# Earlier loads of the scaled SSD output tiles, and one wide stationary block for dt, in a hybrid encoder layer

## The chip, the cores and the metric

The kernel runs on one NeuronCore of a Trainium2 chip. The metric is the device time of one execution in microseconds, as the median of several runs. Engines are called TensorE (PE in the profile, its weight loads PEld), VectorE (DVE), ScalarE (ACT), GpSimd (POOL) and SyncE (SP, which here only issues DMAs).

## The reference

One encoder layer in fp32 is applied to two requests of 256 tokens each, with 1024 channels. Each request goes through a half-step SwiGLU FFN (1024 to 2816 and back), then three branches on the normalised input `u`, then a second FFN:

```
u = rms_norm(x);  q,k,v,q_mem,z,xbc,dt_raw,gates = split(u @ w_in)
A: neighbourhood attention    B: bidirectional Mamba-2 SSD    C: attention into 256 memory tokens
dt_f, dt_b = softplus(dt_raw + bias) ;  a = -exp(a_log)          # 32 heads each, 64 columns in all
y_ssd = ssd(x, dt_f, a_f, B, C) + flip(ssd(flip ...)) + d * x ;  o_ssd = grouped_rms_norm(y_ssd * silu(z))   # 8 groups
merged = sum_b sigmoid(gate_b) * (branch_b @ w_br_b) ;  x = x + merged @ w_out
```

## The kernel before, in words

**Products.** Both requests stand side by side as 512 columns, so tiles are 128 channels by 512 tokens. Every fp32 operand is split into a high part (rounded to fp32r, names ending in h) and the remainder (ending in l), and a product is three fp32r matmuls: high by high, high by low, low by high (`unit`, L535, lines L545 to L547). A unit with 8 blocks of 128 rows is 24 matmuls into one PSUM bank. There are eight banks: five in pool `pm` (names m, q, ac), three in pool `pd` for everything else.

**Weights.** `fetch` (L281) loads weight tiles of up to 128x1024 (`wr`) into a ring of nine, through SP's DMA queue. `ahead` (L312) splits the tiles up to two items ahead: ACT copies to fp32r (`wh`, L322), DVE subtracts for the remainder (`wl`, L236), into pools of three buffers. The subtraction frees the ring slot.

**Order.** `make_plan` (L71) lists the units of TensorE in order. `run` (L361) takes them one after the other. After each unit the last unit's result is evacuated, and `step` (L332) moves each active side task (a generator) to its next `yield` and starts at most one task from a queue. At the `ssd` gates it steps twice per unit (L372), with up to four active tasks (L1029). The instruction order of each engine, SP's DMA issues included, is fixed when the program is built and depends on this order; each engine works in order.

**SSD.** `t_ssd` (L1232) is the side task of a group: decay rows `e` (ACT) are multiplied by dt and by C·B products on DVE, and TensorE turns them into y (L1305). At the end come a sum, a reciprocal root on DVE, and for groups 6 and 7 a diagonal (dg, L514) that TensorE spreads to `R` (L523). For groups 0 to 5 (`KEEP`) the two output tiles go to DRAM (`scr_o`), and so does the factor of the norm (`scr_n`).

**What comes after the last group.** Eight gate units of 24 matmuls (kind `gate`, branch `ssd`, `do_gate` L1026; their tanh `tg` on ACT frees the bank), then 16 units of the branch product (`bs`, L1094) that read all 16 output tiles as pairs `osh`, `osl`. Side task `t_os` (L1340) makes these pairs: for groups 0 to 5 it loads the factor row (`rw`, L1343) and each tile (`or`, L1349), scales the tile on DVE (L247) and splits it (ACT `osh` L258, DVE `osl` L236). It has no step of its own: load, scaling and split are issued at once, tile after tile. Groups 0 to 3 are queued at the first gate (L1029), groups 4 to 7 at the first `bs` unit (L1074).

**dt.** `do_dt` (L1131) is a unit with 64 columns of weights, so 24 matmuls whose result has 64 partitions. `t_dt` (L1138) adds the bias, computes softplus by a series on 64x512 tiles, multiplies by `-exp(a_log)`, then transposes both results in eight 64-row transposes (L1166, L1167) and copies them to `tokd` (128 tokens by four blocks of 128).

**Start.** `warm` (L422) fills a tile on POOL (L425), lets ACT write one column of it (its table load comes first), and runs 16 matmuls on it (L429), 32 passes in the trace, before the first real product (L609).

Of the kernel before, what the change touches and what calls it, by code (L numbers as in the profile page):

```python
# [16 lines left out]
KD = 8  # L17
# [153 lines left out]
PCOLS = {}  # L171
_n = 0
for _name, _w in (("ffn1", 8), ("mix", 8), ("mem", 8), ("ffn2", 8), ("cw", 160), ("cb", 32), ("qn", 1), ("kn", 1),
                  ("mqn", 2), ("mkn", 2), ("sn", 16), ("dd", 16), ("dtb", 1), ("al", 1)):
    PCOLS[_name] = _n
    _n += _w
NPAR = _n
# [7 lines left out]
class Layer:  # L185
# [126 lines left out]
    def ahead(self, ci):  # L312

        for i in range(self.n_split, min(ci + 3, len(ITEMS))):
            it = ITEMS[i]
            self.fetch(i + self.depth)
            self.sums(i + 1)
            n = it.nk * it.m
            t = self.live[it.src]
            hi = self.pw.tile([128, 1024], F32R, tag="hi", name=self.name("wh"))  # L320
# [56 lines left out]
    def setup(self):  # L377
# [3 lines left out]
        dma = nc.sync.dma_start  # L381
# [20 lines left out]
        self.ident, self.ones, self.gele, self.lege = c(0), c(1), c(3, 2), c(6, 2)  # L402
        self.tri = (c(2, 2), c(4, 2))
        self.namask = c(8)[:, :64].rearrange("p (n k) -> p n k", n=2)
        self.lots = self.pc.tile([128, 4, 64], F32, name="lots")
        self.half = self.pc.tile([128, 32], F32, name="half")
        self.merged, self.gus = [None] * 8, {}
# [14 lines left out]
    def warm(self):  # L422

        z = self.g(p="af")
        self.G.memset(z, 0.0)  # L425
        self.act(z[:, :1], z[:, 1:2], AF.Copy)
        ps = self.bank("wm")
        for _ in range(WARM):
            self.T.matmul(ps[:, :256], z[:, :128], z[:, :256], start=True, stop=True)  # L429
# [699 lines left out]


    def do_dt(self, key, cis):  # L1131
        ps = self.unit(cis, self.u, m=64)

        def evac():
            self.later("dt", self.t_dt(ps))
        return evac

    def t_dt(self, ps):  # L1138
        V, S, T = self.V, self.S, self.T
        r = slice(0, 64)  # L1140
        v, m, e, z, w = (self.g(p="dt") for _ in range(5))
        self.act(v[r], ps[r], AF.Identity, bias=self.par("dtb", 0, r))
        self.ts(m[r], v[r], 0.0, ALU.max)
        self.stt(e[r], v[r], -1.0, v[r], ALU.mult, ALU.min)
        self.act(e[r], e[r], AF.Exp)
        yield
        self.ts(w[r], e[r], 2.0, ALU.add)
        V.reciprocal(w[r], w[r])
        self.tt(z[r], e[r], w[r], ALU.mult)
        yield  # L1150
        self.tt(w[r], z[r], z[r], ALU.mult)
        self.ts(e[r], w[r], 1.0 / 15, ALU.mult)
        for k in (13, 11, 9, 7, 5, 3):
            self.stt(e[r], e[r], 1.0 / k, w[r], ALU.add, ALU.mult)
            if k == 9:
                yield
        self.stt(e[r], e[r], 1.0, z[r], ALU.add, ALU.mult)
        self.stt(v[r], e[r], 2.0, m[r], ALU.mult, ALU.add)
        ea = self.small(2, "ea")
        self.act(ea[r, 0:1], self.par("al", 0, r), AF.Exp)  # L1160
        self.ts(w[r], v[r], ea[r, 0:1], ALU.mult, -1.0, ALU.mult)
        yield
        ps = self.bank("dtT")
        for t in range(4):
            s = slice(t * 128, (t + 1) * 128)
            T.transpose(ps[:, t * 128:t * 128 + 64], v[r, s], self.ident[r, 0:64])  # L1166
            T.transpose(ps[:, t * 128 + 64:(t + 1) * 128], w[r, s], self.ident[r, 0:64])  # L1167
        tk = self.pc.tile([128, 4, 128], F32, name="tokd")
        V.tensor_copy(tk.rearrange("p t c -> p (t c)"), ps)
        self.tok = tk  # L1170
# [167 lines left out]
        self.stt(v, v, self.half[:, 2 * g + i:2 * g + i + 1], r, ALU.mult, ALU.mult)  # L1338

    def t_os(self, g):  # L1340
        if g < KEEP:
            r, sn = self.g(p="rw"), self.scr_n
            self.nc.sync.dma_start(out=r, in_=bass.AP(sn.tensor, sn.offset + g * 512, [[0, 128], [1, 512]]))  # L1343
        for i in range(2):
            k = 2 * g + i
            t = self.oraw.pop(k, None)
            if t is None:
                t = self.g(p="or")
                self.nc.sync.dma_start(out=t, in_=self.scr_o[k])  # L1349
                self.scale_o(g, i, t, r)  # L1350
            self.os[k] = self.split_tile(t, "os")
        return
        yield


def layer_kernel(tc, aps):
# [7 lines left out]
def layout(inp):  # L1364
# [15 lines left out]
    def put(name, arr):  # L1380
        p[:arr.shape[0], PCOLS[name]:PCOLS[name] + arr.shape[1]] = arr
# [14 lines left out]
    put("dtb", np.concatenate([f("dt_bias_f")[0], f("dt_bias_b")[0]])[:, None])  # L1396
    put("al", np.concatenate([f("a_log_f")[0], f("a_log_b")[0]])[:, None])

    i = np.arange(128)
    c = np.zeros((128, NCONST), np.float32)  # L1400
# [2 lines left out]
    for k, t in enumerate(tri):  # L1403
# [17 lines left out]
    return {"w": w, "xT": chan("x_prompt", "x_sample"), "memT": chan("mem_prompt", "mem_sample"), "params": p,  # L1421
            "consts": c, "strip": np.ascontiguousarray(strip.reshape(8, 128, 512))}


# [19 lines left out]
```

## Time and profile before

| | |
|---|---|
| median of three runs (lowest, highest) | 1757.79 us (1756.99, 1758.3) |
| the profiled execution | 1756.64 us; its span 1754.9 us |
| granted TensorE clock, mean over the span | 0.998 |
| busy: TensorE, weight loads, DVE, ACT | 1737.2, 1419.9, 1234.6, 848.0 us |
| moved by DMA | 209.69 MB, mean 119 GB/s |

The span runs from the first to the last instruction; the time of the execution adds what lies around it. The busy times overlap, since the engines run side by side. Matmuls are pipelined, so a matmul's row is longer than the distance to the next one; what a matmul costs is read from start to start. In a row of the timeline, the bracket at the end says how long the engine had been idle before it, and what ended that.

### The profile page before, as it was taken

The numbers are of one execution on the slowest core, as the hardware profiler recorded it, in microseconds if no ns is written. First come the engines' busy times: TensorE is split into PE (matmuls) and PEld (weight loads), VectorE is DVE, ScalarE is ACT, GpSimd is POOL, SyncE is SP. The second block draws the span as 40 slices with busy tenths as digits, with TensorE's granted clock in tenths as the row PEclk, the third lists the DMA queues.
The fourth block names the chain that finished last, engine by engine and source line by source line (L and its number), as shares of the span: only waits on it lengthen the run. The fifth ranks groups of instructions, "written<-read, shape, count | busy, mean of one in ns | idle before, by whom it ended". The sixth has DMA issues, their size and how long they took to land.

```text
span 1754.9 us, 22611 instructions
## 1 busy us (share of the span) xinstructions
PE 1737.2 (99%) x8568; PEld 1419.9 (81%) x8568; DVE 1234.6 (70%) x2056; ACT 848.0 (48%) x1515; POOL 0.7 (0%) x5
## 2 busy tenths in 40 slices
PE   9999999999999999999999999999899999999999
PEld 7888888988788888788877777777688878888887
DVE  7676776876544467835778888888753697776775
ACT  6443443543224336533666766766532464444442
POOL 0000000000000000000000000000000000000000
PEclk9999999999999999999999999999999999999999
DMA  6144233442323232333344545446433234244331
GB/s 258 60 143 144 97 107 134 155 156 89 96 77 104 88 103 85 102 109 97 120 127 127 132 139 136 123 138 175 162 126 121 84 109 138 79 153 127 99 115 48
DMA packets 79708, 209.69 MB, mean 119 GB/s; under 512 B 11120, under 2 KB 19696, under 8 KB 79600
## 3 DMA queue, kind: packets, MB, share of 16 engines
q1 hardware_dynamic: 79600, 208.26, 37.6%
q8 instruction: 67, 1.10, 0.3%
q14 instruction: 41, 0.34, 0.1%
HBM read 198.64 MB, written 9.58 MB: 119 GB/s over the span
## 4 chain that ended last, share of the span: by engine, by line
PE 96%; DVE 2%; DMA 1%; ACT 1%; issue 0%; SPq 0%; DVEq 0%; ACTq 0%
PE ac L567 20%; PE m L545 10%; PE m L546 10%; PE m L547 10%; PE q L589 5%; PE q L591 5%; PE q L590 5%; PE m L1094 5%; PE d L546 5%; PE d L547 5%; PE d L545 5%; PE y L1305 2%; PE hT L692 1%; PE CB L1255 1%; PE q L609 1%; PE q L611 1%
## 5 line engine op out<-in xcount | busy, mean ns | idle before, releaser
L322 ACT CAST wh<-wr 128x1024 fp32r<-128x1024 f32 (+1 forms) x357 | 371.2, 1040 | 686.5 <-PE ac L567 167.1
L236 DVE TENSOR_TENSOR wl<-wr,wh 128x1024 fp32r<-128x1024 f32 (+1 forms) x357 | 431.5, 1209 | 264.4 <-ACT wh L322 259.4
L545 PE MATMUL m<-uh,wh 128*128 128x512 f32 (+1 forms) x584 | 234.9, 402 | 6.7 <-ACT tg L251 6.7
L567 PE MATMUL ac<-wh,sh 128*128 128x512 f32 (+1 forms) x616 | 229.4, 373 | 0.5 <-ACT wh L322 0.5
L546 PE MATMUL m<-ul,wh 128*128 128x512 f32 (+1 forms) x584 | 229.6, 393 | 0.0
L567 PE MATMUL ac<-wl,sh 128*128 128x512 f32 (+1 forms) x616 | 228.1, 370 | 0.7 <-DVE wl L236 0.7
L547 PE MATMUL m<-uh,wl 128*128 128x512 f32 (+1 forms) x584 | 228.5, 391 | 0.0
L567 PE MATMUL ac<-wh,sl 128*128 128x512 f32 (+1 forms) x616 | 228.0, 370 | 0.0
L545 PEld LDWEIGHTS m<-uh,wh 128*128 128x128 f32 (+1 forms) x584 | 109.6, 188 | 38.3 <-ACT tg L251 6.9
L546 PE MATMUL d<-hl,wh 128*128 128x512 f32 x352 | 137.2, 390 | 0.7 <-DVE hl L236 0.7
L545 PE MATMUL d<-hh,wh 128*128 128x512 f32 x352 | 137.4, 390 | 0.5 <-ACT hh L258 0.5
L547 PE MATMUL d<-hh,wl 128*128 128x512 f32 x352 | 137.0, 389 | 0.0
L567 PEld LDWEIGHTS ac<-wl,sh 128*128 128x128 f32 x616 | 116.1, 188 | 20.6 <-DVE wl L236 1.3
L567 PEld LDWEIGHTS ac<-wh,sh 128*128 128x128 f32 x616 | 116.0, 188 | 20.6 <-ACT wh L322 1.3
L567 PEld LDWEIGHTS ac<-wh,sl 128*128 128x128 f32 x616 | 116.0, 188 | 19.7
L547 PEld LDWEIGHTS m<-uh,wl 128*128 128x128 f32 (+1 forms) x584 | 109.6, 188 | 24.6 <-issue 0.4
L546 PEld LDWEIGHTS m<-ul,wh 128*128 128x128 f32 (+1 forms) x584 | 109.7, 188 | 23.6 <-issue 1.5
L247 DVE SCALAR_TENSOR_TENSOR x<-d,x 128x512 f32<-128x512 f32 x96 | 66.2, 690 | 76.5 <-PE d L547 76.0
L589 PE MATMUL q<-wh,uh 128*128 128x512 f32 x256 | 102.9, 402 | 0.0
L236 DVE TENSOR_TENSOR wr<-wr,wr 128x1024 f32<-128x1024 f32 x80 | 97.6, 1221 | 6.3 <-DMA wr<-in_w 5.3
L591 PE MATMUL q<-wl,uh 128*128 128x512 f32 x256 | 99.9, 390 | 0.0
L590 PE MATMUL q<-wh,ul 128*128 128x512 f32 x256 | 99.9, 390 | 0.0
(253 smaller groups left out, 2857.6 us busy)
## 6 DMA issues: line engine op xcount, KB each, us to landing
wr<-in_w SPq DMA_DIRECT2D x308, 512.0 KB
rw<-scr_r SPq DMA_DIRECT2D x64, 256.0 KB
nv<-scr_v SPq DMA_DIRECT2D x64, 64.0 KB
scr_o<-cv SPq DMA_DIRECT2D x12, 256.0 KB
or<-scr_o SPq DMA_DIRECT2D x12, 256.0 KB
wr<-in_w SPq DMA_DIRECT2D x9, 256.0 KB
x<-in_xT SPq DMA_DIRECT2D x8, 256.0 KB
mr<-in_memT SPq DMA_DIRECT2D x8, 256.0 KB
```

Of the source, the lines that this page charges most:

```text
L236: self.V.tensor_tensor(out=out, in0=a, in1=b, op=op)
L247: self.V.scalar_tensor_tensor(out=out, in0=a, scalar=s, in1=b, op0=op0, op1=op1)
L322: self.S.copy(hi[:, :n], t[:, :n])
L545: self.T.matmul(ps[:m], wh[:, kk, :], xh, start=i == 0, stop=False)
L546: self.T.matmul(ps[:m], wh[:, kk, :], xl, start=False, stop=False)
L547: self.T.matmul(ps[:m], wl[:, kk, :], xh, start=False, stop=i == n - 1)
L567: go = lambda l, r, **f: self.T.matmul(ps, l, r, skip_group_check=True, **f)
L589: self.T.matmul(self.qb[t], xh, wh[:, kk, :], start=k == 0, stop=False)
L590: self.T.matmul(self.qb[t], xl, wh[:, kk, :], start=False, stop=False)
L591: self.T.matmul(self.qb[t], xh, wl[:, kk, :], start=False, stop=k == KD - 1)
L1094: go = lambda l, r, **f: self.T.matmul(ps, l, r, skip_group_check=True, **f)
L1305: T.matmul(yb[64 * hp:64 * hp + 64, b * 256:(b + 1) * 256], xt[i][:, (2 * b + st) * 128 + 64 * hp:(2 * b + st) * 128 + 64 * hp + 64], w[hp ...
```

## The change

Three things change.

1. `t_os` issues the loads of a group's row and two tiles, yields twice, and only then scales both tiles and splits them. For groups 6 and 7, whose tiles are still on the chip, the split comes at once.
2. For dt, `ahead` puts the high and the low part of the weights side by side in one 128-column stationary block per 128 rows. High by high and low by high are one matmul with 128 output partitions, and high by low a second one with 64. `t_dt` first copies the result out, transposes it in four full transposes, adds both halves and the bias row, and computes softplus on 128 partitions by 256. Bias and `a_log` come as rows, broadcast to all partitions by one DMA at setup (`dtrow`).
3. In `warm`, ACT's column is written in a small tile of its own, filled after the big one, so the matmuls no longer read what ACT writes.

```diff
@@ ahead
+            if it.m == 64:
+                both = self.pw.tile([128, 1024], F32R, tag="hi", name=self.name("wh"))
+                v = both.rearrange("p (k m) -> p k m", k=it.nk)
+                raw = t[:, :n].rearrange("p (k m) -> p k m", k=it.nk)
+                self.S.copy(v[:, :, :64], raw)
+                self.tt(v[:, :, 64:], raw, v[:, :, :64].bitcast(F32), ALU.subtract)
...
@@ setup
+        self.tok = self.pc.tile([128, 4, 128], F32, name="tokd")
+        self.dtrow = self.pc.tile([128, 128], F32, name="dtrow")
+        rows = self.a["dtrow"]
+        dma(out=self.dtrow, in_=bass.AP(rows.tensor, rows.offset, [[0, 128], [1, 128]]))
@@ warm
         self.G.memset(z, 0.0)
-        self.act(z[:, :1], z[:, 1:2], AF.Copy)
+        y = self.small(2, "wm")
+        self.G.memset(y, 0.0)
+        self.act(y[:, :1], y[:, 1:], AF.Copy)
@@ do_dt
-        ps = self.unit(cis, self.u, m=64)
+        ps = self.bank()
+        ci, = cis
+        self.ahead(ci)
+        w = self.split.pop(ci)
+        for k in range(KD):
+            xh, xl = self.u[k]
+            self.T.matmul(ps, w[:, k, :], xh, start=k == 0, stop=False, skip_group_check=True)
+            self.T.matmul(ps[:64], w[:, k, :64], xl, start=False, stop=k == KD - 1, skip_group_check=True)
@@ t_dt (the series itself is as before, on 128x256)
-        v, m, e, z, w = (self.g(p="dt") for _ in range(5))
-        self.act(v[r], ps[r], AF.Identity, bias=self.par("dtb", 0, r))
+        raw = self.g(p="dt")
+        S.copy(raw, ps)
+        yield
+        ps = self.bank("dtT")
+        for t in range(4):
+            c = slice(t * 128, (t + 1) * 128)
+            T.transpose(ps[:, c], raw[:, c], self.ident)
+        v, m, e, z, w = (self.g(p="dt")[:, :256] for _ in range(5))
+        self.tt(four(v), four(ps)[:, :, 0:64], row(0), ALU.add)
+        self.tt(four(v), four(ps)[:, :, 64:128], four(v), ALU.add)
...
-        self.act(ea[r, 0:1], self.par("al", 0, r), AF.Exp)
-        self.ts(w[r], v[r], ea[r, 0:1], ALU.mult, -1.0, ALU.mult)
-        yield
-        ps = self.bank("dtT")
-        for t in range(4):
-            s = slice(t * 128, (t + 1) * 128)
-            T.transpose(ps[:, t * 128:t * 128 + 64], v[r, s], self.ident[r, 0:64])
-            T.transpose(ps[:, t * 128 + 64:(t + 1) * 128], w[r, s], self.ident[r, 0:64])
-        tk = self.pc.tile([128, 4, 128], F32, name="tokd")
-        V.tensor_copy(tk.rearrange("p t c -> p (t c)"), ps)
+        self.stt(tk[:, :, 0:64], four(e), 2.0, four(m), ALU.mult, ALU.add)
+        self.act(self.dtrow[:, 64:], self.dtrow[:, 64:], AF.Exp)
+        self.stt(tk[:, :, 64:128], tk[:, :, 0:64], -1.0, row(1), ALU.mult, ALU.mult)
@@ t_os
+        ks = (2 * g, 2 * g + 1)
         if g < KEEP:
             r, sn = self.g(p="rw"), self.scr_n
             self.nc.sync.dma_start(out=r, in_=bass.AP(sn.tensor, sn.offset + g * 512, [[0, 128], [1, 512]]))
-        for i in range(2):
-            k = 2 * g + i
-            t = self.oraw.pop(k, None)
-            if t is None:
-                t = self.g(p="or")
-                self.nc.sync.dma_start(out=t, in_=self.scr_o[k])
-                self.scale_o(g, i, t, r)
-            self.os[k] = self.split_tile(t, "os")
-        return
-        yield
+            for k in ks:
+                self.oraw[k] = self.g(p="or")
+                self.nc.sync.dma_start(out=self.oraw[k], in_=self.scr_o[k])
+            yield
+            yield
+            for i in range(2):
+                self.scale_o(g, i, self.oraw[ks[i]], r)
+        for k in ks:
+            self.os[k] = self.split_tile(self.oraw.pop(k), "os")
```

The first place where rows move is ACT's queue during the last gate units. `tg_..<-m_..` is a gate's tanh, `osh` the cast of an output tile, `wh` that of a weight tile, `yq` and `e` belong to the last SSD groups. Before, from the fifth early tile to the seventh gate's tanh:

```order
L258 CAST osh_10877<-or_10874 128x512
L322 CAST wh_11103<-wr_10555 128x1024
L251 ACTIVATE yq_11033<-cv_10453 128x512
L258 CAST osh_10884<-or_10881 128x512
L322 CAST wh_11136<-wr_10557 128x1024
L258 CAST osh_10915<-or_10912 128x512
L258 CAST osh_10922<-or_10919 128x512
L251 ACTIVATE tg_10957<-m_10824 128x512
L251 ACTIVATE tg_11020<-m_10926 128x512
L251 ACTIVATE tg_11066<-m_10989 128x512
L251 ACTIVATE tg_11131<-m_11035 128x512
L251 ACTIVATE tg_11164<-m_11100 128x512
```

With the change, from the third gate's tanh to the eighth early tile:

```order
L251 ACTIVATE tg_10929<-m_10796 128x512
L251 ACTIVATE e_10936<-e_10936 128x256
L251 ACTIVATE e_10964<-rw_10860,lots 128x256 x2
L251 ACTIVATE e_10936<-rw_10860,lots 128x128
L258 CAST osh_10946<-or_10856 128x512
L251 ACTIVATE e_10936<-rw_10860,lots 128x128
L251 ACTIVATE e_10964<-e_10964 128x512
L258 CAST osh_10950<-or_10858 128x512
L251 ACTIVATE e_10936<-e_10936 128x256
L332 CAST wh_11030<-wr_10545 128x1024
L258 CAST osh_10973<-or_10894 128x512
L258 CAST osh_10977<-or_10896 128x512
```

The tanh of the third gate (tg_10957 before, tg_10929 now) stood behind the casts of all eight early tiles and now stands ahead of the last four; those of the fourth to sixth gate follow behind the next weight cast after the piece shown.

The second place is SP's queue in the same stretch. `or` are output tiles, `rw` rows of the norm (scr_n) or of the SSD (scr_r), `wr` weight tiles. Before, from the fifth early tile to the eighth:

```order
L1349 DMA or_10874<-scr_o 128x512
L290 DMA wr_11101<-in_w 128x1024
L1349 DMA or_10881<-scr_o 128x512
L290 DMA wr_11134<-in_w 128x1024
L1349 DMA or_10912<-scr_o 128x512
L1343 DMA rw_11230<-scr_n 128x512
L1343 DMA rw_11277<-scr_n 128x512
L290 DMA wr_11169<-in_w 128x1024
L1349 DMA or_10919<-scr_o 128x512
```

With the change, from an SSD row to the first weight loads after the eighth early tile:

```order
L1254 DMA rw_10829<-scr_r 128x512
L1369 DMA rw_10854<-scr_n 128x512
L1254 DMA rw_10860<-scr_r 128x512
L1372 DMA or_10856<-scr_o 128x512
L1372 DMA or_10858<-scr_o 128x512
L1369 DMA rw_10892<-scr_n 128x512
L1372 DMA or_10894<-scr_o 128x512
L1372 DMA or_10896<-scr_o 128x512
L290 DMA wr_10982<-in_w 128x1024
L290 DMA wr_11028<-in_w 128x1024
L290 DMA wr_11093<-in_w 128x1024
L290 DMA wr_11126<-in_w 128x1024
```

Before, a weight load stood ahead of each of these tiles; now the fifth to eighth tile (or_10856 to or_10896) stand together, ahead of the weight loads (wr_10982 is the tile that was wr_10990). The loads of the first four early tiles likewise stand together, a few rows higher up.

The third place is the dt unit on TensorE. Before, the first six of 24 rows:

```order
L545 MATMUL m_3790<-uh_3206,wh_3724 64x512
L546 MATMUL m_3790<-ul_3207,wh_3724 64x512
L547 MATMUL m_3790<-uh_3206,wl_3725 64x512
L545 MATMUL m_3790<-uh_3213,wh_3724 64x512
L546 MATMUL m_3790<-ul_3214,wh_3724 64x512
L547 MATMUL m_3790<-uh_3213,wl_3725 64x512
```

With the change, the first six of 16:

```order
L1155 MATMUL m_3794<-uh_3211,wh_3729 128x512
L1156 MATMUL m_3794<-ul_3212,wh_3729 64x512
L1155 MATMUL m_3794<-uh_3218,wh_3729 128x512
L1156 MATMUL m_3794<-ul_3219,wh_3729 64x512
L1155 MATMUL m_3794<-uh_3259,wh_3729 128x512
L1156 MATMUL m_3794<-ul_3260,wh_3729 64x512
```

The third row of each block of 128 is gone, and the first has 128 output partitions.

## Rows read from the trace of the kernel before

**Rows 1.** The page's busy times in us (share of the span, number of instructions).

```profile
PE 1737.2 (99%) x8568; PEld 1419.9 (81%) x8568; DVE 1234.6 (70%) x2056; ACT 848.0 (48%) x1515; POOL 0.7 (0%) x5
```

**Rows 2.** All that TensorE waited for from 1196 to 1300 us: us in total, times, longest.

```profile
PE m L545 <- ACT tg L251: 6.7, 1, 6.7
PE R L523 <- DVE dg L514: 0.5, 1, 0.5
```

**Rows 3.** Timeline of the last gate units, by engine: start in us, duration in us, engine, line, operation, tiles, count, idle before.

```profile
1261.53 0.33 SPq L290 DMA_DIRECT2D wr<-in_w  x1
1261.92 2.52 SPq L1349 DMA_DIRECT2D or<-scr_o  x2
...
1265.77 0.75 DVE L247 SCALAR_TENSOR_TENSOR or<-or,half,rw 128x512 f32<-128x512 f32 x1 [1.68 <-DMA or<-scr_o]
...
1266.56 0.62 ACT L258 CAST osh<-or 128x512 fp32r<-128x512 f32 x1 [3.74 <-DVE or L247]
1267.08 2.54 ACT L251 ACTIVATE tg<-m 128x512 f32<-128x512 f32 x5
...
1259.87 1.13 PE L523 MATMUL R<-dg,consts 128*128 128x128 f32 x8 [0.48 <-DVE dg L514]
1267.72 0.79 PE L545 MATMUL m<-uh,wh 128*128 128x512 f32 x1 [6.72 <-ACT tg L251]
...
1271.26 0.39 PE L547 MATMUL m<-uh,wl 128*128 128x512 f32 x1
```

**Rows 4.** The second half of the stall, and the stretch after it: length, busy us (instructions) of PE, PEld, DVE, ACT, POOL, then the granted clock, the DMA share and GB/s.

```profile
1264.40:1267.70 3.30, 0.00 (x0) 0.00 (x0) 1.24 (x2) 1.14 (x3) 0.00 (x0) 0.50 0.49 160
1267.70:1271.26 3.56, 3.54 (x9) 2.81 (x9) 0.20 (x1) 1.92 (x4) 0.00 (x0) 0.51 0.00 0
```

**Rows 5.** SP's queue some 30 us earlier, as a timeline: the first and the last of five issues.

```profile
1230.98 0.33 SPq L290 DMA_DIRECT2D wr<-in_w  x1
...
1233.27 0.44 SPq L1349 DMA_DIRECT2D or<-scr_o  x1
```

**Rows 6.** Timeline of DVE, and of TensorE at two groups of y matmuls, in the same stretch.

```profile
1239.70 0.69 DVE L236 TENSOR_TENSOR osl<-or,osh 128x512 fp32r<-128x512 f32 x1
1240.31 0.48 DVE L247 SCALAR_TENSOR_TENSOR e<-e,tokd,ca 128x256 f32<-128x256 f32 x1
1240.70 0.61 DVE L247 SCALAR_TENSOR_TENSOR e<-e,tokd,cb 128x128 f32<-128x128 f32 x2
1241.23 1.22 DVE L236 TENSOR_TENSOR wl<-wr,wh 128x1024 fp32r<-128x1024 f32 x1
1242.37 0.42 DVE L236 TENSOR_TENSOR e<-e,e 128x256 f32<-128x256 f32 x1
...
1243.10 0.74 DVE L247 SCALAR_TENSOR_TENSOR or<-or,half,rw 128x512 f32<-128x512 f32 x1
...
1239.33 0.65 PE L1305 MATMUL y<-e,xt 128*64 128x256 f32 x2
1239.90 0.50 PE L546 MATMUL m<-ul,wh 128*128 128x512 f32 x1
...
1243.57 1.08 PE L1305 MATMUL y<-e,xt 128*64 128x256 f32 x6
```

**Rows 7.** What the weight casts on ACT waited for from 1196 to 1300 us, the largest entry.

```profile
ACT wh L322 <- PE m L546: 15.4, 7, 5.2
```

**Rows 8.** Timeline of TensorE around the dt unit and the unit behind it, around dt's transposes, and around four full transposes elsewhere.

```profile
455.53 0.40 PE L545 MATMUL m<-uh,wh 128*64 128x512 f32 x1
...
461.05 0.39 PE L589 MATMUL q<-wh,uh 128*128 128x512 f32 x1
...
466.49 0.39 PE L589 MATMUL q<-wh,uh 128*128 128x512 f32 x1
...
493.78 0.27 PE L1166 MATMUL dtT<-consts,dt 64*128 64x64 f32 x1
...
494.42 0.50 PE L589 MATMUL q<-wh,uh 128*128 128x512 f32 x1
...
402.79 1.18 PE L836 MATMUL tr<-consts,kr 128*128 128x128 f32 x8
403.72 0.48 PE L589 MATMUL q<-wh,mgh 128*128 128x512 f32 x1
```

**Rows 9.** DVE's copy of dt's result as a timeline row, and the stretch from 440 to 520 us with the columns of rows 4.

```profile
494.52 0.69 DVE L1169 COPY tokd<-dtT 128x512 f32<-128x512 f32 x1 [3.42 <-PE dtT L1167]
...
440.00:520.00 80.00, 80.00 (x374) 64.42 (x373) 42.49 (x67) 21.53 (x39) 0.00 (x0) 1.00 0.29 88
```

**Rows 10.** The start as a timeline, and two stretches of the warm-up matmuls alone (length, PE, PEld, clock, DMA share, GB/s).

```profile
0.73 0.52 POOL L425 MEMSET af<- 128x512 f32 x1 [0.29 <-POOLq L1428]
...
2.02 0.20 ACT L251 ACTIVATE af<-af 128x1 f32<-128x1 f32 x1
...
2.28 10.11 PE L429 MATMUL wm<-af 128*128 128x256 f32 x32 [2.28 <-ACT af L251]
...
7.56 1.23 DVE L236 TENSOR_TENSOR wl<-wr,wh 128x1024 fp32r<-128x1024 f32 x1 [0.84 <-ACT wh L322]
...
2.28:8.28 6.00, 6.00 (x14) 4.79 (x15) 1.00 0.94 321
8.28:12.04 3.76, 3.76 (x19) 3.27 (x18) 1.00 1.03 404
```

More of the change, by code (lines that the diff above doesn't have):

```diff
@@ L173 @@
 for _name, _w in (("ffn1", 8), ("mix", 8), ("mem", 8), ("ffn2", 8), ("cw", 160), ("cb", 32), ("qn", 1), ("kn", 1),
-                  ("mqn", 2), ("mkn", 2), ("sn", 16), ("dd", 16), ("dtb", 1), ("al", 1)):
+                  ("mqn", 2), ("mkn", 2), ("sn", 16), ("dd", 16)):
     PCOLS[_name] = _n
@@ L319, in ahead @@
             t = self.live[it.src]
+            if it.m == 64:
[4 more added lines that the diff above has]
+                self.tt(v[:, :, 64:], raw, v[:, :, :64].bitcast(F32), ALU.subtract)
+                self.drop(it.src)
+                self.split[i] = v
+                self.n_split = i + 1
+                continue
             hi = self.pw.tile([128, 1024], F32R, tag="hi", name=self.name("wh"))
@@ L1140, in t_dt @@
         r = slice(0, 64)
-        v, m, e, z, w = (self.g(p="dt") for _ in range(5))
-        self.act(v[r], ps[r], AF.Identity, bias=self.par("dtb", 0, r))
-        self.ts(m[r], v[r], 0.0, ALU.max)
-        self.stt(e[r], v[r], -1.0, v[r], ALU.mult, ALU.min)
-        self.act(e[r], e[r], AF.Exp)
-        yield
-        self.ts(w[r], e[r], 2.0, ALU.add)
-        V.reciprocal(w[r], w[r])
-        self.tt(z[r], e[r], w[r], ALU.mult)
-        yield
[L1151 to L1159, printed above, removed]
-        self.act(ea[r, 0:1], self.par("al", 0, r), AF.Exp)
-        self.ts(w[r], v[r], ea[r, 0:1], ALU.mult, -1.0, ALU.mult)
+        four = lambda z: z.rearrange("p (t c) -> p t c", t=4)
+        raw = self.g(p="dt")
+        S.copy(raw, ps)
         yield
@@ L1164, in t_dt @@
         for t in range(4):
-            s = slice(t * 128, (t + 1) * 128)
-            T.transpose(ps[:, t * 128:t * 128 + 64], v[r, s], self.ident[r, 0:64])
-            T.transpose(ps[:, t * 128 + 64:(t + 1) * 128], w[r, s], self.ident[r, 0:64])
-        tk = self.pc.tile([128, 4, 128], F32, name="tokd")
-        V.tensor_copy(tk.rearrange("p t c -> p (t c)"), ps)
-        self.tok = tk
+            c = slice(t * 128, (t + 1) * 128)
+            T.transpose(ps[:, c], raw[:, c], self.ident)
+        v, m, e, z, w = (self.g(p="dt")[:, :256] for _ in range(5))
+        tk = self.tok
+        row = lambda i: self.dtrow[:, 64 * i:64 * i + 64].unsqueeze(1).to_broadcast([128, 4, 64])
+        self.tt(four(v), four(ps)[:, :, 0:64], row(0), ALU.add)
+        self.tt(four(v), four(ps)[:, :, 64:128], four(v), ALU.add)
+        self.ts(m, v, 0.0, ALU.max)
+        self.stt(e, v, -1.0, v, ALU.mult, ALU.min)
+        self.act(e, e, AF.Exp)
+        yield
+        self.ts(w, e, 2.0, ALU.add)
+        V.reciprocal(w, w)
+        self.tt(z, e, w, ALU.mult)
+        yield
+        self.tt(w, z, z, ALU.mult)
+        self.ts(e, w, 1.0 / 15, ALU.mult)
+        for k in (13, 11, 9, 7, 5, 3):
+            self.stt(e, e, 1.0 / k, w, ALU.add, ALU.mult)
+            if k == 9:
+                yield
+        self.stt(e, e, 1.0, z, ALU.add, ALU.mult)
+        self.stt(tk[:, :, 0:64], four(e), 2.0, four(m), ALU.mult, ALU.add)
+        self.act(self.dtrow[:, 64:], self.dtrow[:, 64:], AF.Exp)
+        self.stt(tk[:, :, 64:128], tk[:, :, 0:64], -1.0, row(1), ALU.mult, ALU.mult)
         yield
@@ L1343, in t_os @@
             self.nc.sync.dma_start(out=r, in_=bass.AP(sn.tensor, sn.offset + g * 512, [[0, 128], [1, 512]]))
-        for i in range(2):
-            k = 2 * g + i
-            t = self.oraw.pop(k, None)
-            if t is None:
-                t = self.g(p="or")
-                self.nc.sync.dma_start(out=t, in_=self.scr_o[k])
-                self.scale_o(g, i, t, r)
-            self.os[k] = self.split_tile(t, "os")
-        return
-        yield
+            for k in ks:
+                self.oraw[k] = self.g(p="or")
+                self.nc.sync.dma_start(out=self.oraw[k], in_=self.scr_o[k])
+            yield
+            yield
+            for i in range(2):
+                self.scale_o(g, i, self.oraw[ks[i]], r)
+        for k in ks:
+            self.os[k] = self.split_tile(self.oraw.pop(k), "os")
 def layer_kernel(tc, aps):
@@ L1395, in layout @@
     put("dd", cols(np.repeat(f("ssd_d")[0], 64)))
-    put("dtb", np.concatenate([f("dt_bias_f")[0], f("dt_bias_b")[0]])[:, None])
-    put("al", np.concatenate([f("a_log_f")[0], f("a_log_b")[0]])[:, None])
+    dtrow = np.concatenate([f(n)[0] for n in ("dt_bias_f", "dt_bias_b", "a_log_f", "a_log_b")])
     i = np.arange(128)
@@ L1420, in layout @@
     strip = strip.reshape(8, 2, 128, 256).transpose(0, 2, 1, 3)
-    return {"w": w, "xT": chan("x_prompt", "x_sample"), "memT": chan("mem_prompt", "mem_sample"), "params": p,
+    return {"w": w, "xT": chan("x_prompt", "x_sample"), "memT": chan("mem_prompt", "mem_sample"), "params": p, "dtrow": dtrow,
             "consts": c, "strip": np.ascontiguousarray(strip.reshape(8, 128, 512))}
```

## Prediction, made before the changed kernel ran

> **What bounds the kernel now.** I began with the page's busy times and its chain of waits. TensorE is busy for 1737.2 of 1754.9 us [rows 1], and the chain runs through it nearly all the way. So only two things shorten this kernel: fewer TensorE instructions, or less than the 17.7 us in which it idles. Time on other engines counts only where TensorE waits for it. The list of its waits names two in the stretch of the output tiles [rows 2]: 6.7 us once, for a gate's tanh on ACT, and 0.5 us for the diagonal of a group norm. A third, 2.28 us, stands at the start [rows 10].
>
> Then I read the timeline around the 6.7 us [rows 3]. TensorE's R matmuls start at 1259.87; the next gate unit starts only at 1267.72. It needs a PSUM bank, and a gate's bank comes free by its tanh. Five tanh run together from 1267.08, right behind the cast of an output tile (osh, 1266.56). That cast waited for the scaling (or, 1265.77), and the scaling 1.68 us more for its load. The load was one of two issued from 1261.92, right behind a weight load at 1261.53, which had waited for a ring slot that DVE's weight remainder frees. So a 256 KB load stood in SP's queue behind a weight load that goes at TensorE's own pace, and the tanh stood behind the tile in ACT's queue.
>
> The stall also costs clock: the granted clock is 0.50 in its second half and 0.51 in the 3.56 us in which work goes on [rows 4], the lower of the two levels (1.2 GHz), until about 1271.26.
>
> **Cost 1: loads two steps ahead.** The same 12 tile loads, 6 row loads, 12 scalings and 12 splits are issued; only their places move. In the new SP order all eight early tiles stand ahead of the weight load that is issued at 1230.98 now [rows 5], so the eighth, one of the two at 1261.92 now, is asked for nearly 30 us earlier. In the new ACT order the third gate's tanh, which frees the last gate's bank, comes before the last four of the eight casts instead of behind all. I expect the whole stall to go: 6.72 us of idling, and the slow stretch after it. From 1267.72 to 1271.26 eight matmuls ran in 3.54 us [rows 3]; at full clock 24 take 461.05 to 466.49, 0.227 us each [rows 8], so eight are 1.82. That is 1.72 more: **8.4 us**. Nor does a DVE remainder stand between sum and diagonal any more (0.61 us, [rows 6]), so of the 0.48 us wait before R [rows 3] most should go: **0.4 us**.
>
> What is late next? Weight loads now stand behind tile loads in SP's queue. I cost that at nothing: the weight casts of this stretch waited for TensorE to give buffers back [rows 7], not for loads, as the ring of nine runs ahead. Without that cover the delay would be eight tile issues of 0.44 us each [rows 5]. Dearer is the DVE order: scalings and remainders of two tiles now come in pairs between the sums that feed the y matmuls. By start-to-start distance [rows 6] a remainder takes 0.61 (1239.70 to 1240.31), a pair of 256-column products 0.78, a pair of 128-column ones 0.53, a weight remainder 1.14; a sum and a scaling, 0.08 less than their rows like these, 0.34 and 0.66; I count the gating of a y tile like a remainder. Between the four sums that the last y tile needs, the new order makes DVE do 5.9, 4.2 and 5.8 us, 15.9 in all. On TensorE one y matmul (two passes) holds the stream for 0.57 us (1239.33 to 1239.90), and three, by the longer row, for about 1.0. Between the same y matmuls it has 24, 16 and 25 unit matmuls and one, three and one of y: 6.0, 4.6 and 6.3, in all 16.9. So DVE is nearly as full as TensorE for 16 us. The first sum should be ready some 1.7 us before its y (13 unit matmuls, 2.95 us, against 0.66 and 0.34 for scaling the y tile and the sum, and hand-overs of 0.1 to 0.2 like that from DVE to PE at the end of the stall), and part of that lead goes where remainders wait for casts. I take no new wait; bounds 0 and 2 us.
>
> **Cost 2: dt.** The unit drops from 24 matmuls to 16. The 24 with 64 columns run from 455.53 to 461.05, 0.230 each, as far apart as the 128-column ones behind them (0.227) [rows 8]: the width costs nothing, the count does. Eight fewer: 1.84 us. The eight 64-row transposes hold the stream from 493.78 to 494.42, 0.64 us; four full ones, two passes each, hold it as at 402.79 to 403.72, 0.93 us [rows 8]. Net **1.6 us**; bounds 1.4 and 1.9.
>
> Softplus on 128 partitions halves the rows' length on DVE. An ACT copy, two additions and a broadcast load come in; two activations, a scaling and the last copy go. I cost all this at nothing: TensorE was busy for the whole of 440 to 520 us while DVE had 42.5 and ACT 21.5 us of work [rows 9]. The new additions wait for transposes in TensorE's queue, with a weight remainder behind them; now the tokd copy waits there 3.42 us [rows 9] and nobody waits for it, so the upper bound is a wait of that size, and I take zero. The broadcast load is one more issue on SP early in the first block, 0.33 to 0.44 us like those of [rows 5]; the weight loads behind it move by that much, under a ring of nine.
>
> **Cost 3: the warm-up.** Its matmuls waited for an ACT instruction behind a table load: the fill ends at 1.25, the activation starts at 2.02, TensorE at 2.28 [rows 10]. Now they wait for the fill alone. With the 0.06 us that lie between activation and TensorE now that is 1.31, 0.97 earlier. The first real operands are ready (wl ends at 8.79) long before the warm-up ends at 12.04, so an earlier end is a real gain. Its size depends on the clock: the first 6.0 us hold 14 warm-up rows, the next 3.76 us hold 19 [rows 10]. The granted clock reads 1.00 in both, so here the pace tells of the slower level, not the record. If the slow stretch ends as much earlier as it begins, the gain is 0.97. If its end stays at 8.28, TensorE does 0.97/0.43 = 2.3 matmuls more by then, each worth 0.20 at full pace: 0.45. I take **0.7 us**, between the two, as no row prefers either. The Trainium skill (TensorE: Matmul & The Clock Gate, part 1, on the HAM clock gate) says that the window behind the gate runs freely, whenever the kernel starts, and that the slow start is a span of time and not a number of matmuls; by that rule the slow stretch need not move with the start, and with its end left in place the sum would be 10.9 instead of 11.1. This trace shows the change of pace once, so it cannot tell.
>
> **Sum.** 8.4 + 0.4 + 1.6 + 0.7 = 11.1 us. The profiled execution took 1756.64 us (span 1754.9), which gives 1745.5. It lies 1.15 below the median of the runs, 1757.79, which gives 1746.7. Leaning a little to the profiled run, from which all terms come, I forecast **1746.5 us** for a median.
>
> **Rivals.**
> - *DVE takes over in the tail.* The y matmuls or a weight remainder come late by more than the lead. For: 15.9 against 16.9 us, and remainders that wait for casts. Against: there is no TensorE wait for DVE over 0.5 us in this stretch now [rows 2], with the same work on DVE. Each late microsecond is one of TensorE; with 2 to 6 us in all, 1748.5 to 1752.5.
> - *The stall moves and nothing of it is won* (the change does not do what it says). The next bank taken, that of the first bs unit, is freed by the fourth gate's tanh, still behind eight casts. It stalls if the eighth tile is late. Against: that tile is asked for nearly 30 us earlier. Then only dt and warm-up pay: 1757.8 - 2.3 = 1755.5.
> - *Slower: DVE holds a late tile in front of the sums.* The eighth tile's scaling stands ahead of the products of the last sum, in order. The first of the four y groups stands six unit matmuls earlier than the one at 1239.33 [rows 6], so the last is due near 1254.8 on today's scale, with 5.8 us of DVE from that scaling on before it. A landing after about 1249 decides: from there on the last y, and with it the gate unit, waits as long. To lose all 11.1 us and 3.5 more takes a wait of about 13 us and the 1.7 us that the lower clock adds, so a landing after 1262. What could do it is the row load ahead of it in SP's queue, which waits for ACT to release a slot. Time: 1762. Against: now five issues, row loads among them, go out within 2.3 us there [rows 5], so slots are free.
>
> **How the numbers follow.** A measurement here tells changes of 0.2% (3.5 us) apart. Forecast 0.70; DVE in the tail 0.17; stall moved 0.09; slower 0.04. The low end is all upper bounds from the profiled time: 8.4 + 0.5 + 1.9 + 1.0 = 11.8, 1744.8. The high end takes in the lower bounds (1.4, 0.45, 2 us of new waits, no gain at R: 1749.6 from the median) and the first third of the DVE rival: 1750.2. That leaves out some 2 in 10. Faster by over 0.2% (below 1754.3) are the first two cases and little else: 0.87; within, 0.09; slower, 0.04.
>
> **What would show it.** Right: no TensorE wait of microseconds for a tanh; granted clock 1.00 throughout 1240 to 1280; TensorE's idle time down from 17.7 to about 9.5 us; 16 dt matmuls; warm-up from about 1.3. The forecast is wrong if TensorE waits for e, for a weight remainder or for a tanh for over 2 us between the last y tile and the first bs units, if warm-up still ends near 12.0, or if weight casts in the first block wait for loads.

## The result, and the profile after

| kernel | median (lowest to highest), us | against the kernel before on the same chip |
|---|---|---|
| changed, first set | 1743.99 (1742.89 to 1744.78) | 1757.39; ratio 0.9923 [0.9906, 0.9940] |
| changed, second set | 1743.60 (1742.64 to 1744.50) | 1757.67; 0.9918 [0.9905, 0.9932] |
| changed, third set | 1744.03 (1743.05 to 1744.56) | 1757.18; 0.9925 [0.9911, 0.9938] |

The change is faster by 13.1 to 14.1 us, 0.8%. The forecast was 1746.5 with a low end of 1744.8, so the direction held and the result lies 0.8 us below the range. The gain was sized too small. Below are the rows of the changed kernel that answer to the rows ahead. First the page's busy times, and the largest of TensorE's waits over the whole span (us in total, times, longest):

```profile
PE 1731.4 (99%) x8556; PEld 1417.2 (81%) x8556; DVE 1227.9 (71%) x2057; ACT 846.6 (49%) x1515; POOL 0.8 (0%) x6
```

```profile
PE wm L445 <- POOL wm L441: 1.3, 1, 1.3
PE d L562 <- DVE hl L236: 0.7, 2, 0.4
PE qT L967 <- DVE nt L247: 0.7, 1, 0.7
PE kT L975 <- DVE kr L236: 0.7, 1, 0.7
PE ac L583 <- DVE wl L236: 0.7, 1, 0.7
PE ns L997 <- ACT npT L1025: 0.5, 1, 0.5
```

The waits for the tanh and for the diagonal [rows 2] are gone. TensorE idles 1741.1 - 1731.4 = 9.7 us of its span instead of 17.7. The wait `ns` for `npT` near 673 us, in a part that the change does not touch, is new in this trace; it comes back below. The stretch of the stall, with the columns of [rows 4], is full and at full clock:

```profile
1240.00:1262.00 22.00, 22.00 (x104) 16.40 (x105) 16.77 (x39) 9.68 (x16) 0.00 (x0) 1.00 0.43 130
1262.00:1280.00 18.00, 18.00 (x81) 14.90 (x80) 13.26 (x18) 7.62 (x11) 0.00 (x0) 1.00 0.40 135
```

SP's queue as a timeline shows why. The last four early tiles go out from 1225.41 to 1229.76, ahead of five weight loads whose issues then stretch over 20 us. On ACT, the tanh of the gates no longer stand behind all eight casts:

```profile
1225.41 1.62 SPq L1372 DMA_DIRECT2D or<-scr_o  x2
1227.13 0.52 SPq L1369 DMA_DIRECT2D rw<-scr_n  x1
1227.70 2.06 SPq L1372 DMA_DIRECT2D or<-scr_o  x2
1236.13 20.31 SPq L290 DMA_DIRECT2D wr<-in_w  x5
...
1237.24 0.57 ACT L251 ACTIVATE tg<-m 128x512 f32<-128x512 f32 x1
1239.12 0.60 ACT L258 CAST osh<-or 128x512 fp32r<-128x512 f32 x1
1240.45 0.60 ACT L258 CAST osh<-or 128x512 fp32r<-128x512 f32 x1
1243.06 0.62 ACT L258 CAST osh<-or 128x512 fp32r<-128x512 f32 x1 [0.75 <-DVE or L247]
1244.06 0.62 ACT L258 CAST osh<-or 128x512 fp32r<-128x512 f32 x1 [0.38 <-DVE or L247]
1248.04 1.56 ACT L251 ACTIVATE tg<-m 128x512 f32<-128x512 f32 x3
```

The start, the dt unit with the unit behind it, and dt's transposes, as timelines of TensorE; ahead of them the first real product of the kernel before:

```profile
12.04 0.59 PE L609 MATMUL q<-wh,sh 128*128 128x512 f32 x1
```

```profile
1.31 8.63 PE L445 MATMUL wm<-af 128*128 128x256 f32 x32 [1.31 <-POOL wm L441]
9.59 0.58 PE L625 MATMUL q<-wh,sh 128*128 128x512 f32 x1
...
452.89 0.39 PE L1155 MATMUL m<-uh,wh 128*128 128x512 f32 x1
456.60 0.39 PE L605 MATMUL q<-wh,uh 128*128 128x512 f32 x1
...
472.93 0.60 PE L1172 MATMUL dtT<-consts,dt 128*128 128x128 f32 x4
473.28 0.48 PE L605 MATMUL q<-wh,uh 128*128 128x512 f32 x1
```

The warm-up starts 0.97 us earlier, as forecast, but the first real product comes 2.45 earlier (9.59, 12.04 before). The dt unit takes 3.71 us (5.52 before): 1.81 less, 1.84 forecast. The four full transposes hold TensorE's stream for 0.35 us, where the forecast had 0.93. The first real product lay furthest from the forecast, so the start was the first suspect: theory A takes the warm-up term as mis-sized, and its rival B takes the early end of the slow pace as a chance of this one execution.

### The profile page after: what moved, and what is told of

The parts are those of the page before. It is cut to its first block, busy times and chain, and to the rows that moved or that the text cites. A ratio compares the mean times of both kernels' runs of the same rounds, so it can differ in the third digit from the quotient of the medians.

```text
span 1741.1 us, 22593 instructions
## 1 busy us (share of the span) xinstructions
PE 1731.4 (99%) x8556; PEld 1417.2 (81%) x8556; DVE 1227.9 (71%) x2057; ACT 846.6 (49%) x1515; POOL 0.8 (0%) x6
## 4 chain that ended last, share of the span: by engine, by line
PE 98%; DVE 1%; ACT 1%; issue 0%; POOL 0%; DVEq 0%; ACTq 0%; POOLq 0%
PE ac L583 21%; PE m L561 10%; PE m L562 10%; PE m L563 10%; PE q L605 5%; PE m L1110 5%; PE q L607 5%; PE q L606 5%; PE d L562 5%; PE d L563 5%; PE d L561 5%; PE y L1330 2%; PE hT L708 1%; PE CB L1280 1%; PE am L865 1%; PE amo L893 1%
## 5 line engine op out<-in xcount | busy, mean ns | idle before, releaser
L561 PE MATMUL m<-uh,wh 128*128 128x512 f32 x576 | 230.8, 401 | 0.0
L562 PE MATMUL m<-ul,wh 128*128 128x512 f32 x576 | 225.5, 392 | 0.0
L563 PE MATMUL m<-uh,wl 128*128 128x512 f32 x576 | 225.2, 391 | 0.0
L561 PEld LDWEIGHTS m<-uh,wh 128*128 128x128 f32 x576 | 108.2, 188 | 30.0 <-ACT wh L332 5.4
L563 PEld LDWEIGHTS m<-uh,wl 128*128 128x128 f32 x576 | 108.1, 188 | 24.8 <-issue 1.5
L562 PEld LDWEIGHTS m<-ul,wh 128*128 128x128 f32 x576 | 108.3, 188 | 22.0 <-issue 0.8
```

The costliest lines, as they stand in the source:

```text
L561: self.T.matmul(ps[:m], wh[:, kk, :], xh, start=i == 0, stop=False)
L562: self.T.matmul(ps[:m], wh[:, kk, :], xl, start=False, stop=False)
L563: self.T.matmul(ps[:m], wl[:, kk, :], xh, start=False, stop=i == n - 1)
```

## The experiments

Ratios are given as [95% interval]; an interval is some 3 to 6 us wide here. Terms under a microsecond are settled by the traces, with the times as support.

**One part at a time.** The three parts of the diff, each put alone into the kernel before, and the changed kernel without its warm-up part. The edits are pieces of the diff above:

```diff
e1_warm:     before + @@ warm
e2_os:       before + @@ t_os
e3_dt:       before + @@ ahead, setup, do_dt, t_dt
e4_no_warm:  before + @@ t_os, ahead, setup, do_dt, t_dt
```

> The kernel before with the change of the warm-up alone. Theory A (the warm-up term was mis-sized: TensorE starts 0.97 us earlier, and the slow pace of its first matmuls ends earlier by about 3 us with it): first real product near 9.6 us instead of 12.04, and about 2.4 us less than before. Theory B (the end of the slow pace falls by chance, and the profiled execution of the changed kernel drew an early one): first product somewhere between 9.6 and 11.6, and in the median 0.45 to 0.97 us less than before, the bounds of the prediction.

> The kernel before with the earlier tile loads alone. Both theories: the 6.72 us wait and the stretch at granted clock 0.50 go, nothing new in their place; 9.2 us less than before (the shift between the first y and the first bs unit in the two traces), where the prediction had 8.8. Start and dt as before: first product near 12.0 by theory A; by theory B it may lie anywhere from 10.5 to 12.

> The kernel before with the dt change alone. Both theories: dt unit 3.7 us instead of 5.5 (1.8 less), and the transposes 0.35 us instead of 0.64 (0.3 less, where the prediction had 0.29 more): about 2.1 us less than before. The 6.72 us wait stays. Start as in the kernel before, as for the run with the tile loads alone.

> The changed kernel with its warm-up put back to the old form. Theory A: about 2.4 us more than the changed kernel (11.3 less than before), first product near 12.0. Theory B: 0.45 to 0.97 us more than the changed kernel, first product anywhere from 10.5 to 12.

All four ran beside the kernel before at 1756.87:

| kernel | median, us | less than before | forecast by the prediction | ratio |
|---|---|---|---|---|
| e1_warm | 1756.19 | 0.7 | 0.7 | 0.9995 [0.9986, 1.0003] |
| e2_os | 1746.92 | 9.95 | 8.8 | 0.9942 [0.9930, 0.9955] |
| e3_dt | 1754.22 | 2.65 | 1.6 | 0.9985 [0.9976, 0.9993] |
| e4_no_warm | 1744.34 | 12.5 | 10.4 | 0.9927 [0.9914, 0.9941] |

The times speak against theory A. The first product of e1_warm does come at 9.64, but the runs gain 0.7 us, not 2.4; the interval reaches from 0.5 more to 2.5 less, so 2.4 lies at its very end. The timeline of e1_warm's TensorE shows where most of the rest went (1.3 us): it now waits for a weight remainder and for the norm's squares, which it did not before.

```profile
10.90 0.50 PE L613 MATMUL q<-wl,sh 128*128 128x512 f32 x1 [0.47 <-DVE wl L236]
39.90 1.05 PE L508 MATMUL sum<-consts,sq 128*128 128x1 f32 x8 [0.83 <-DVE sq L236]
```

Theory B named a chance in the start, and the same 32 warm-up passes took 8.63 to 9.41 us in six profiles with the new start and 9.13 to 10.22 in six with the old. So the slow pace does end at different times. The means of the first product are 9.95 and 11.84, so 2.45 is more than a usual pair of executions differs by. But the undersized terms were the other two, and both theories had left those alone.

**What the stall costs.** The stall was in e1_warm and e3_dt as well, and their traces differ in what follows it. Windows of e3_dt with the columns of [rows 4]:

```profile
1265.28:1267.70 2.42, 2.41 (x6) 1.93 (x7) 0.19 (x1) 1.91 (x4) 0.00 (x0) 0.50 0.00 0
1267.70:1270.60 2.90, 2.90 (x9) 2.22 (x8) 0.00 (x0) 0.00 (x0) 0.00 (x0) 0.50 0.00 0
1270.60:1275.00 4.40, 4.40 (x21) 3.65 (x20) 0.58 (x1) 1.54 (x2) 0.00 (x0) 0.99 0.00 0
```

Its TensorE resumes at 1265.29 and the next matmul at full pace starts at 1270.58:

```profile
1265.29 0.79 PE L559 MATMUL m<-uh,wh 128*128 128x512 f32 x1 [6.77 <-ACT tg L251]
...
1270.58 0.44 PE L559 MATMUL m<-uh,wh 128*128 128x512 f32 x1
```

These are twelve slow matmuls in 5.29 us, which at 0.227 each would be 2.72: 2.6 us lost. In the profiled run of the kernel before it was eight, and 1.7 lost. In e1_warm it is again eight in 3.50 us (1.7 lost), in `f7_row` below fourteen in 6.07 (2.9 lost). The idle time ahead of them is the same, 6.72 to 6.83 us. The run lists say the same: of the 60 runs of the kernel before beside the experiments, 34 have a mean granted clock of 0.997 and a median of 1757.6 us, 26 have 0.998 and 1756.7; in each of the four sets the first group is the slower one, by 0.5 to 1.1. The profiled runs with eight slow matmuls (before, e1_warm) have 0.998, those with twelve and fourteen (e3_dt, f7_row) 0.997. Theory C, that the low clock costs the median run more than the profiled one, was tested by keeping TensorE busy through the stall:

```diff
@@ do_gate
+        if key == ("ssd", 7):
+            pf = self.bank("fill")
+            xh = self.u[0][0]
+            for _ in range(26):
+                self.T.matmul(pf, xh[:, :128], xh, start=True, stop=True)
         ps = self.unit(cis, self.u)
```

> The kernel before, with 26 matmuls (128x512, 0.227 us each, 5.9 in all) put between R and the last gate unit, into a free bank that nobody reads: TensorE works through most of its 6.7 us wait. Their result is not used. Theory C (the stall costs its idle time and then a slow stretch whose length differs between executions, 1.7 us or about 2.9): the wait stays as a wait of some 0.8 us, the granted clock stays 1.00 in every run, the median falls by 1.7 to 2.9, most likely 2.3, and the spread of the runs shrinks. Theory D (the slow stretch costs 1.72 always; the rest of the difference lies elsewhere): 1.7 less, spread as before.

> The changed kernel once more, beside the others of this set on one chip. 1743 to 1744; if the slow stretch behind the stall is what made the earlier set's gain larger than the profiled execution's sum (theory C), all its runs have a mean granted clock of 1.000, while those of the kernel before are divided between 0.997 and 0.998.

The median was 1755.22 against 1757.67 (ratio 0.9988 [0.9979, 0.9997]): 2.45 us less. The gate unit still starts as late as its tanh lets it (7.80 us behind the start of R, 7.85 before); only the clock differs. The timeline row of the filler, the wait that is left, and windows from the stall on:

```profile
1261.87 6.19 PE L1036 MATMUL fill<-uh 128*128 128x512 f32 x26
1268.79 0.50 PE L545 MATMUL m<-uh,wh 128*128 128x512 f32 x1 [0.73 <-ACT tg L251]
```

```profile
1264.40:1267.70 3.30, 3.30 (x17) 2.69 (x15) 1.56 (x3) 0.08 (x1) 0.00 (x0) 1.00 0.77 283
1267.70:1271.26 3.56, 2.83 (x13) 2.02 (x12) 0.69 (x1) 2.99 (x6) 0.00 (x0) 1.00 0.00 0
```

All eleven runs have a mean clock of 1.000, as have the five of the changed kernel. So by these runs the low clock costs 2.45 us in the median where 1.72 was forecast, with an interval from 0.5 to 3.7. The size alone does not exclude D's 1.7; the four traces (1.7 to 2.9) and the two groups of runs do, and they speak for C. One expectation of C failed: the spread did not shrink (1753.84 to 1756.36), so the length of the low clock is not all that differs between runs. The profiled execution, the slowest of the eleven, shows one more such thing:

```profile
673.07 1.09 PE L981 MATMUL ns<-kT,qbd 64*64 64x128 f32 x22 [1.06 <-ACT npT L1009]
```

This wait is absent in the trace of before, 0.3 to 0.9 us in five others and 1.06 here. It does not go with any of the edits: of the changed kernel's three traces two show it, with 0.5 and 0.3 us, and the third does not.

**Is it the distance of two steps?** The changed kernel without the yields: both loads of a pair, then both scalings at once.

```diff
@@ t_os
-            yield
-            yield
             for i in range(2):
                 self.scale_o(g, i, self.oraw[ks[i]], r)
```

> The changed kernel without the two yields in the loading of output tiles: both loads of a pair are issued together, and both scalings at once behind them. Theory P (what pays is that a pair's two loads no longer stand behind the first tile's scaling and a weight load): no TensorE wait of microseconds, time within 1 us of the changed kernel, though DVE waits 1 to 3 us for a tile. Theory Q (the distance of two steps pays): DVE's scalings wait 2 to 3 us per pair for their loads, in front of the sums that y needs, and TensorE with them: 2 to 8 us more than the changed kernel.

The median was 1744.11 (ratio 0.9922 [0.9909, 0.9936]), 0.5 above the changed kernel beside it. No long wait came back. These are the waits from 1196 to 1300 us in it, TensorE's and DVE's for the factor rows:

```profile
PE R L539 <- DVE dg L530: 0.4, 1, 0.4
PE y L1330 <- ACT wh L332: 0.3, 1, 0.3
```

```profile
DVE or L247 <- DMA rw<-scr_n: 2.3, 2, 1.7
```

And its SP queue, the last four early tiles:

```profile
1230.53 1.11 SPq L1372 DMA_DIRECT2D or<-scr_o  x2
1231.74 0.46 SPq L1369 DMA_DIRECT2D rw<-scr_n  x1
1233.21 2.21 SPq L1372 DMA_DIRECT2D or<-scr_o  x2
1247.12 10.78 SPq L290 DMA_DIRECT2D wr<-in_w  x4
```

P held. The two loads of a pair still go out together, and the last four tiles stand together ahead of the four weight loads of the last row, where before a weight load stood ahead of each tile. DVE now waits up to 1.7 us for a row, and TensorE waits 0.7 us in this stretch that it does not wait in the changed kernel; that the one comes from the other is not shown. What pays is the place of the loads, not the distance of two steps.

**The transposes.** Each of dt's four issued four times:

```diff
         for t in range(4):
             c = slice(t * 128, (t + 1) * 128)
-            T.transpose(ps[:, c], raw[:, c], self.ident)
+            for _ in range(4):
+                T.transpose(ps[:, c], raw[:, c], self.ident)
```

> The changed kernel, as the yardstick for the two others of this set on the same chip. 1743 to 1744; first real product between 9.6 and 10.3 us, as in its two profiles.

> The changed kernel with each of dt's four full transposes issued four times into the same place, 12 more. If four hold TensorE's stream for 0.35 us, as read from the trace of the changed kernel, the next matmul comes 1.05 us later and the time rises by 1.05; if for 0.93, as the prediction had it, by 2.8.

```profile
473.73 1.91 PE L1173 MATMUL dtT<-consts,dt 128*128 128x128 f32 x16
475.39 0.47 PE L605 MATMUL q<-wh,uh 128*128 128x512 f32 x1
```

Sixteen hold the stream for 1.66 us, four for 0.35: 1.3 more in the trace. The median, 1744.91 (ratio 0.9931 [0.9919, 0.9943]), is 0.9 above the changed kernel; the interval is too wide to decide by the time alone, the trace does. A full transpose costs about 0.1 us, not 0.23.

**The rest of dt.** Unit and transposes make 1.81 + 0.29 = 2.1 of the 2.65 us. In the trace of before, TensorE waits twice near 59 us for DVE's product `sg` of the first block, as in e1_warm, e2_os and f1_fill, and in no trace with the new dt:

```profile
58.80 0.66 PE L692 MATMUL hT<-consts,sg 128*128 128x128 f32 x4 [0.28 <-DVE sg L247]
60.59 0.44 PE L692 MATMUL hT<-consts,sg 128*128 128x128 f32 x2 [0.21 <-DVE sg L247]
```

The build puts `t_dt`'s exponential on the row tile, which waits for nothing but its load, some thirty rows into ACT's queue (at 22 to 26 us in the traces), and the first two `sg` products in DVE's queue move back, behind weight additions `wr` that do not wait for ACT. The kernel before with these alone:

```diff
@@ setup
+        self.dtrow = self.pc.tile([128, 128], F32, name="dtrow")
+        rows = self.a["dtrow"]
+        dma(out=self.dtrow, in_=bass.AP(rows.tensor, rows.offset, [[0, 128], [1, 128]]))
@@ t_dt
+        self.act(self.dtrow[:, 64:], self.dtrow[:, 64:], AF.Exp)
         ea = self.small(2, "ea")
```

> The kernel before with two things of the dt change that should cost nothing: the broadcast load of the row tile at setup, and an exponential on it (64 columns) that nobody reads, which the build puts near the start of ACT's queue and which moves two of DVE's products (sg) by one to three places in the first block. All else as before. Theory G (the dt change gained about 0.5 us that way, besides its matmuls): the two TensorE waits of hT for sg near 59 and 61 us, 0.49 together, go, and the time falls by 0.3 to 0.5. Theory H (those waits fell out for another reason, as the start's own jitter): the waits stay, time as before within 0.2.

The median was 1756.32 against 1757.21 (ratio 0.9995 [0.9986, 1.0004]). The interval takes in no change, but the trace is clear: the same transposes follow each other without a wait, also with the start of the kernel before. DVE had waited 0.77 us for ACT's `sg` with two additions behind it; now the additions come first. DVE's rows, before and in f7_row:

```profile
54.39 0.75 DVE L247 SCALAR_TENSOR_TENSOR sg<-up,rfffn,sg 128x512 f32<-128x512 f32 x1 [0.77 <-ACT sg L251]
```

```profile
55.54 2.07 DVE L247 SCALAR_TENSOR_TENSOR sg<-up,rfffn,sg 128x512 f32<-128x512 f32 x3
```

TensorE in f7_row:

```profile
57.62 0.82 PE L695 MATMUL hT<-consts,sg 128*128 128x128 f32 x6
59.47 0.44 PE L695 MATMUL hT<-consts,sg 128*128 128x128 f32 x2
...
1266.65 0.79 PE L548 MATMUL m<-uh,wh 128*128 128x512 f32 x1 [6.79 <-ACT tg L251]
...
1272.72 0.39 PE L550 MATMUL m<-uh,wl 128*128 128x512 f32 x1
```

(The last two rows are the first and the next full-pace matmul behind its stall, used above.) How much it is worth shows from the block's first `ac` matmul to the first of the dt unit, here before and in f7_row (the dt unit of before starts at 455.53 [rows 8]):

```profile
56.77 0.39 PE L567 MATMUL ac<-wh,sh 128*128 128x512 f32 x1
```

```profile
56.26 0.39 PE L570 MATMUL ac<-wh,sh 128*128 128x512 f32 x1
454.38 0.40 PE L548 MATMUL m<-uh,wh 128*64 128x512 f32 x1
```

That is 398.76 and 398.12 us. The four traces without the row tile have 398.69 to 398.76, the ten with it 398.09 to 398.15, whatever their start. So G's mechanism holds in every trace and H's does not: 0.6 us, 0.49 of it waiting, came with an edit in another place. Whether the load or the exponential moved the rows was not separated, and the time of f7_row alone (0.9 less) would not exclude H.

**What a microsecond at the start is worth.** The changed kernel with 22 warm-up matmuls, and another with 13 in the same place:

```diff
-RING, DEPTH, WARM = 9, 8, 16
+RING, DEPTH, WARM = 9, 8, 22
```

> The changed kernel with 22 warm-up matmuls instead of 16: 12 passes more of 0.21 us, first real product near 12.1 instead of 9.6. Theory E (an earlier first product is partly given back within the first 40 us, where the norm's sum waits for DVE): 0.4 to 1.9 us more, by the runs with and without the warm-up change most likely 0.7. Theory F (a microsecond at the start is one at the end): 2.5 us more.

> The changed kernel with 13 warm-up matmuls instead of 16, six passes fewer (1.27 us at full pace). The first product then waits for its operands, whose last is ready at 9.50 us in the trace of the changed kernel: 0.1 to 0.8 us earlier than with 16, depending on when the slow pace ends. Theory E (start time is partly given back): 0 to 0.5 us less than the changed kernel. Rival: the pause of up to 1.2 us ahead of the first product costs more than it saves.

With 22 the first product came at 12.91 instead of 10.29, and the median at 1745.59 (ratio 0.9931 [0.9919, 0.9944]): by the medians 2.0 of the 2.6 us arrive at the end, just above the range of E and nearer to F than the forecast of 0.7. The two traces give less: the first `ac` matmul of the block comes 1.55 us later (57.60 and 56.05), as the changed kernel waits 0.8 us for the norm's squares there and the kernel with 22 does not. So part is given back, as E says; how much, these runs do not settle. With 13 the first product came at 9.19 instead of 10.19, and the median at 1743.07 (0.9923 [0.9911, 0.9936]), 1.0 below the changed kernel, with runs from 1742.92 to 1745.75. This is more than E's 0 to 0.5 and no pause ahead of the first product shows, but it is within what can be told from no change, so it is no proven improvement.

## Why the prediction was right in kind and too small

| term | predicted | what the runs and traces show |
|---|---|---|
| stall, idle | 6.72 | gone whole |
| low clock behind it | 1.72 | 1.7, 1.7, 2.6, 2.9 in four traces; 2.45 by the filler |
| wait before R | 0.4 | 0.48, gone |
| dt unit | 1.84 | 1.81 |
| dt transposes | -0.29 | +0.29 (0.64 to 0.35) |
| first block, by dt's row tile | 0 | 0.64 (0.49 of it waiting) |
| warm-up | 0.7 | 0.7 alone; 2.45 at the first product, partly given back |
| sum | 11.1 | 13.1; runs 13.1 to 14.1 |

- **Mechanism: right.** The tile loads left the weight loads behind, the tanh left the casts behind, the wait went, and nothing took its place. None of the rivals came. DVE in the tail stayed under TensorE: in the trace TensorE has not one wait for it from 1196 to 1300 us. Whether the margin was the one worked out was not measured.
- **The step that failed is the low clock's term in cost 1, and the sum built on it.** "From 1267.72 to 1271.26 eight matmuls ran": that length belongs to one execution, and was priced as if to the kernel. The prediction saw that the profiled execution lay 1.15 us below the median and split the difference. But by the two groups of runs 0.9 of such a gap is the longer low clock of the other runs, and the change takes it away in every run. The consistent base was the profiled execution (1745.5), and leaning to the median was the wrong direction: of the 2.5 us between forecast and median, 1.0 is that lean. Another 1.2 us is cost 2, in the next two points; with 0.1 at R, some 0.2 is left. With the terms as measured in that execution (12.4 in all) the count down gives 1744.3, against 1744.0. The Trainium skill (TensorE: Matmul & The Clock Gate, part 1, on the HAM clock gate) says of a kernel's start that the same kernel shows different numbers of slow matmuls from run to run, since the gate's window runs freely. The traces here agree for the start (8.63 to 10.22 us for the same passes) and show the like behind a stall in the middle: 8, 8, 12 and 14 slow matmuls behind nearly equal idle times. The prediction had used that rule for the start alone.
- **Cost 2, the transposes:** the row with eight entries [rows 8] was read as four transposes of two passes. It is eight of one pass, as the row of the changed kernel with four entries for four transposes shows. The sign was wrong by that: 0.29 gained instead of lost.
- **Cost 2, the cover:** the row tile's load and exponential were costed at nothing since TensorE was busy from 440 to 520 us. The exponential does not run there: the build moved it into the first 26 us, and with it DVE's order near 55 us, where TensorE did wait. The order of ACT and DVE in that place could be read before any run.
- **Cost 3:** the median came out as forecast by luck, from two errors against each other. The earlier start was worth more at the first product than the upper bound of 0.97, since the slow pace also ended earlier, and part of it was given back at the waits of the first 40 us. The premise that the operands are ready long before does not hold: the first remainder `wl` ends at 8.79 in the trace of before, but at 9.50 in that of the changed kernel and at 10.85 in e1_warm's, behind its first product.
- **Two slips of the sums** change nothing: by its own terms the high end is 1749.5 and not 1749.6, and the slower rival 1761 and not 1762.

What stays open: the terms name 13.1 of 13.1 to 14.1 us, and the rest is within the intervals; the two that rest on medians alone, low clock and warm-up, are known to about 2 us. What sets where the low clock ends was not tried.

## What to carry to other kernels

Read a stall's price from several executions: its idle time repeats, the low clock behind it need not. If a change removes the stall, count down from the profiled execution in which all its terms were read, and do not lean back to a median that holds other lengths of the same loss. In the same way, settle terms under a microsecond by one stretch that all traces share (here 398.7 against 398.1 us), not by the medians. When the build sets the order, look where a new instruction without dependencies lands, since its price or gain is there and not where the code stands.

## What the runs showed of the hardware

- Filling a wait with useless matmuls bought back 2.45 us without shortening the wait: the granted clock stayed at 1.00 instead of 0.50 (2.4 instead of 1.2 GHz).
- The same 32 warm-up passes took from 8.63 to 10.22 us over twelve profiles.
- Behind stalls of 6.72 to 6.83 us, 8 to 14 matmuls ran at the low clock (1.7 to 2.9 us lost).
- Full fp32 transposes (128x128) follow each other at about 0.1 us: sixteen held TensorE's stream for 1.66 us.
